# A transformer block's down projection on one core: closing sums moved to GpSimd behind the weights' sums, lower rows first, one scaling operation per row

## The chip, the cores and the metric

The kernel runs on one core of a Trainium2 chip. The metric is device time in microseconds (us). The time before is 1584.97 us, the median of three runs (1581.94 to 1589.53). One further execution was profiled; all durations below come from it. Engines: PE is TensorE's matmul (PEld its weight load), DVE is VectorE, ACT is ScalarE, POOL is GpSimd, SP is SyncE, which here only issues DMAs.

## The reference, cut to what matters

The kernel computes one decoder block for a sequence of 1024 tokens and a model width of 1024: a state-space branch and an attention branch, merged and projected, and then a feed-forward part. The change lies in the last two lines:

```python
h = modulate(rmsnorm(x, norm2_g[l]), sh2, sc2)
ffn = (jax.nn.silu(h @ w_ffn_gate[l]) * (h @ w_ffn_up[l])) @ w_ffn_down[l]
x = x + g2 * ffn
return rmsnorm(x, norm_f_g)
```

The hidden width is 2816, that is 22 blocks of 128. `g2` is one row of 1024 values and is multiplied into the rows of `w_ffn_down`, so that the projection can be added to `x` directly. The final `rmsnorm` scales each row of the output by one number (the reciprocal root of its mean square) and by the row `gf`, which holds `norm_f_g`.

## The kernel before

Only `down` (from line 1164 on) and a few tables above it matter here. Every fp32 matrix product is made of three matmuls: each operand is split into a rounded high part (`h`, cast on ACT) and a rest (`l`, the difference, on DVE), and `PRODUCTS` multiplies high by high, high by rest and rest by high.

**Seven products in place of eight.** The output is cut into four quadrants of 512 rows by 512 columns: upper rows (row tiles 0 to 3, of 128 rows each) and lower rows (4 to 7), left and right columns. Twenty of the hidden blocks are taken in ten pairs. For each pair seven products of sums of blocks replace eight products of blocks. The sums on the activations' side are read from memory (`hD`, line 1203). The sums on the weights' side are made on POOL (line 1211, one operation of 128x512), except for products 2 and 5, which need none. Then come ACT's cast (line 1212, or 1208) and DVE's difference (line 1213, or 1209).

**Three steps.** `STEPS = (4, 3, 3)` deals the ten pairs out over three passes. In each pass the seven products are run in the order `ORDER = (2, 4, 5, 3, 1, 6, 7)`. For one product in the last pass, PE makes four output tiles of nine matmuls each (line 1220), 36 matmuls, and DVE adds each finished tile to that product's accumulator (line 1226). The accumulators are named `pb` (products 4, 5, 7) and `x` (2, 3, 1, 6) in the trace; the listings of instructions number them: `x_9958` and `x_9959` are product 2, `x_9960` and `x_9961` product 3, `x_9962` and `x_9963` product 1, `x_9964` and `x_9965` product 6, two tiles in each.

**The closing sums.** The quadrants are sums of accumulators. In the last pass each product's tiles are followed by the sums that have become possible (line 1230), 32 operations of 128x512:

```python
CLOSE = ((2, 6, 2, ALU.subtract), (4, 2, 4, ALU.add), (4, 7, 4, ALU.add), (5, 7, 5, ALU.subtract),
         (3, 6, 3, ALU.add), (3, 3, 5, ALU.add), (1, 6, 1, ALU.add), (1, 7, 1, ALU.add))
TENG = (6, 7)
```

An entry (z, o, a, op) says: behind product z, accumulator o takes in accumulator a. The entries whose numbers stand in `TENG`, the two that take in product 1, run on DVE, the others on POOL. At the end the upper quadrants are in accumulators 7 and 3, the lower ones in 2 and 6.

**The row loop** (from line 1256 on). The two hidden blocks that are left get four plain operands (lines 440 and 441, `operand`). For each row tile t from 0 to 7, PE makes two tiles of six matmuls (line 1268) and DVE adds each to its quadrant (line 1270). ACT squares the row and sums it (line 1278), POOL multiplies the row by `gf` (line 1251), and `rstd` makes the row's scale from the sum with a few 128x1 operations on DVE (lines 450, 456, 460, 461) and ACT (453, 454). DVE multiplies the row by it (line 1253) and SP writes the row out (line 1254). The scaling of a row is written behind the first half of the next one. The last row does its halves apart (lines 1246 to 1249, 1272 and 1274).

Each engine runs its instructions in a fixed order. A scheduler sets that order when the kernel is built, from the order in the code, the priorities and the buffers; an instruction that waits holds up all behind it on its engine.

Of the kernel before, what the change touches and what calls it, by code (L numbers as in the profile page):

```python
# [9 lines left out]
F32 = mybir.dt.float32  # L10
# [3 lines left out]
ALU = mybir.AluOpType  # L14
# [14 lines left out]
class S5:  # L29
# [244 lines left out]
    def run(self, m, tabs, u_src, y_dst):  # L274
# [55 lines left out]
        for j in range(8):  # L330
# [4 lines left out]
P = 128  # L335
KT = 8
# [24 lines left out]
SIGN_A = {i: ALU.subtract if i in (6, 7) else ALU.add for i in range(1, 8)}  # L361
SIGN_B = {i: ALU.subtract if i in (3, 4) else ALU.add for i in range(1, 8)}

CLOSE = ((2, 6, 2, ALU.subtract), (4, 2, 4, ALU.add), (4, 7, 4, ALU.add), (5, 7, 5, ALU.subtract),
         (3, 6, 3, ALU.add), (3, 3, 5, ALU.add), (1, 6, 1, ALU.add), (1, 7, 1, ALU.add))
SLOT = {3: 0, 6: 1, 7: 2, 4: 3, 1: 4, 2: 5, 5: 6}

BENG = {(i, j, e) for i in range(1, 8) for j in range(2) for e in range(2) if j or not e or i == 6}
# [1 line left out]

STEPS = (4, 3, 3)

TENG = (6, 7)


class Turns:

# [15 lines left out]
class Block:  # L393
# [674 lines left out]
    def gate_up(self, pair, wv, tp):  # L1068
# [3 lines left out]
        for x, y in ((1, 0), (1, 1), (0, 0), (0, 1)):  # L1072
            t = A[x, y] = self.W.tile([P, 2, 4, P], F32, name="wb")
            for q in range(2):
# [87 lines left out]
    def down(self, const, tp, g2, gf):  # L1162

        nc = self.nc
        w_v = self.i["w_ffn_down"][0].rearrange("(m p) n -> m p n", p=P)
        x_v = self.xD.rearrange("(t p) n -> p t n", p=P)
        flat = lambda t: t.rearrange("p a b -> p (a b)")
        L, R = slice(0, 512), slice(512, 1024)
        ring = self.wring + [(self.F, t, t) for t in ("f0", "f0", "f1", "f1")]
        self.turn = 0  # L1170
        acc = {}
        for i in (4, 5, 7, 2, 3, 1, 6):
            pool, tag = (self.PB, "pb") if i in (4, 5, 7) else (self.X, "x1")
            acc[i] = [pool.tile([P, 2, 512], F32, name=tag) for _ in range(2)]
            if i in FROM:
                x, y = FROM[i]
                for a in range(2):
                    nc.sync.dma_start(out=acc[i][a], in_=x_v[:, 4 * x + 2 * a:4 * x + 2 * a + 2, 512 * y:512 * y + 512])
        for i, op in ((5, ALU.add), (4, ALU.subtract)):
            for a in range(2):  # L1180
                nc.gpsimd.tensor_tensor(flat(acc[7][a]), flat(acc[7][a]), flat(acc[i][a]), op)

        def tiles():
            pool, ht, lt = ring[self.turn % len(ring)][0:3]
            self.turn += 1
            return pool.tile([P, 1024], F32R, name=ht), pool.tile([P, 1024], F32R, name=lt)

        def weights(m):
            w = self.PA.tile([P, 1024], F32, name="pa")
            nc.sync.dma_start(out=w, in_=w_v[m])  # L1190
            nc.gpsimd.tensor_tensor(w, w, g2, ALU.mult)  # L1191
            return w

        p0 = 0
        stages = Turns(*[(self.W, "wb", 4)] * 4, *self.stages.pools)
        for s, np_ in enumerate(STEPS):
            W = [(weights(2 * p), weights(2 * p + 1)) for p in range(p0, p0 + np_)]
            for n, i in enumerate(ORDER):
                ops = []
                (ay, ax), b = TERMS_B[i]  # L1200
                for p in range(np_):
                    st = stages.tile([P, 1024], F32)
                    nc.sync.dma_start(out=st[:, L], in_=self.hD[p0 + p, :, SLOT[i]])
                    u = W[p][ay][:, 512 * ax:512 * ax + 512]
                    h, l = tiles()
                    if b is None:
                        for q, v in ((L, st[:, L]), (R, u)):
                            nc.scalar.copy(h[:, q], v)
                            nc.vector.tensor_tensor(l[:, q], v, h[:, q].bitcast(F32), ALU.subtract)  # L1209
                    else:  # L1210
                        nc.gpsimd.tensor_tensor(st[:, R], u, W[p][b[0]][:, 512 * b[1]:512 * b[1] + 512], SIGN_B[i])  # L1211
                        nc.scalar.copy(h, st)
                        nc.vector.tensor_tensor(l, st, h.bitcast(F32), ALU.subtract)  # L1213
                    ops.append((h, l))
                for t in range(4):
                    ps = self.banks.tile([P, 512], F32)
                    j = 0
                    for o in ops:
                        for x, y in PRODUCTS:
                            nc.tensor.matmul(ps, lhsT=o[x][:, P * t:P * t + P], rhs=o[y][:, R], start=(j == 0), stop=(j == 3 * np_ - 1))  # L1220
                            j += 1
                    m = {z: acc[z][t // 2][:, t % 2] for z in acc}
                    if s == 0 and i not in FROM:
                        (nc.scalar.copy if (n * 4 + t) % 2 else nc.vector.tensor_copy)(m[i], ps)
                    else:
                        nc.vector.tensor_tensor(m[i], ps, m[i], ALU.add)  # L1226
                    if s == len(STEPS) - 1:
                        for c, (z, o, a, op) in enumerate(CLOSE):
                            if z == i:
                                (nc.vector if c in TENG else nc.gpsimd).tensor_tensor(m[o], m[o], m[a], op)  # L1230
            p0 += np_
        ops = []
        for m in range(2):
            st = self.W.tile([P, 1024], F32, name="wb", bufs=4)
            nc.sync.dma_start(out=st, in_=self.lD[m])
            ops.append((self.operand(st, tiles=tiles()), self.operand(weights(20 + m), tiles=tiles())))
        out = self.out.rearrange("o (t p) d -> p (o t) d", p=P)
        L, R = slice(0, 512), slice(512, 1024)

        def at(t):  # L1240
            return lambda n: small[:, t, "vya".index(n) + 2:"vya".index(n) + 3]

        def close(t, row, ss):
            if t == 7:
                r = self.rstd(const, ss[:, 1:2], 1, ss[:, 0:1], at(t))
                nc.scalar.mul(row[:, L], row[:, L], r)
                nc.vector.scalar_tensor_tensor(row[:, R], row[:, R], r, gf[:, R], ALU.mult, ALU.mult)
                for cs in (L, R):
                    nc.sync.dma_start(out=out[:, t, cs], in_=row[:, cs])
                return  # L1250
            nc.gpsimd.tensor_tensor(row, row, gf, ALU.mult)
            r = self.rstd(const, ss[:, 0:1], 1, None, at(t))
            nc.vector.tensor_scalar(row, row, r, None, ALU.mult)
            nc.sync.dma_start(out=out[:, t], in_=row)

        small = const.tile([P, KT, 5], F32, name="ss3")
        last = None
        for t in range(KT):
            ss = small[:, t, 0:2]
            row = self.PA.tile([P, 1024], F32, name="pa")  # L1260
            sq = tp.tile([P, 1024], F32, name="ft")
            for c in range(2):
                cs = slice(512 * c, 512 * c + 512)
                ps = self.banks.tile([P, 512], F32)
                j = 0
                for h, w in ops:
                    for x, y in PRODUCTS:
                        nc.tensor.matmul(ps, lhsT=h[x][:, P * t:P * t + P], rhs=w[y][:, cs], start=(j == 0), stop=(j == 5))
                        j += 1
                nc.vector.tensor_tensor(row[:, cs], ps, acc[((7, 3), (2, 6))[t // 4][c]][t % 4 // 2][:, t % 2], ALU.add)  # L1270
                if t == 7:
                    nc.scalar.activation(sq[:, cs], row[:, cs], AF.Square, accum_out=ss[:, c:c + 1])
                    if c == 0:
                        nc.gpsimd.tensor_tensor(row[:, cs], row[:, cs], gf[:, cs], ALU.mult)
                if c == 0 and last:
                    close(*last)
            if t != 7:
                nc.scalar.activation(sq, row, AF.Square, accum_out=ss[:, 0:1])
            last = (t, row, ss)
        close(*last)  # L1280

    def run(self):
        tc, nc, i = self.tc, self.nc, self.i
        with ExitStack() as es:
# [77 lines left out]
            with ExitStack() as s4:  # L1362
                self.X = s4.enter_context(self.pool("x1", KT, side="right"))
                self.F = s4.enter_context(self.pool("f", 4, side="right"))
                self.W = s4.enter_context(self.pool("wb", 4, side="right"))
                wx = s4.enter_context(self.pool("wx", 1, side="right"))
# [44 lines left out]
```

## Time and profile before

| | before |
|---|---|
| median of three runs | 1584.97 us |
| the profiled execution's own time | 1583.8 us |
| its span in the profile | 1582.1 us |
| PE busy | 1424.0 us (90%) |
| DVE busy | 1094.8 us (69%) |
| POOL busy | 821.3 us (52%) |
| ACT busy | 616.2 us (39%) |
| start of the last product's stall on PE | 1519.2 us |
| first add of the row loop on DVE | 1544.77 us |

The span is the stretch from the first to the last thing that the profile recorded; the execution's own time is 1.7 us longer. Busy shares are means over stages with different limits, so the end of the program has to be read from its own stretch, from about 1509 us on. In the rows below a time is counted from the span's start, a duration in a timeline is in us and in a group of instructions in us and in ns, and what stands in square brackets is the idle time of the engine ahead of that row and what ended it.

### The profile page before, as it was taken

Reading aid. Unit: us, or ns where it says so; the run is one execution under the profiler, and the core shown is the slowest. Engines: PE = TensorE matmul, PEld = TensorE weight load, DVE = VectorE, ACT = ScalarE, POOL = GpSimd, SP = SyncE. Lnnn points to the kernel's source line nnn. Section 1 sums busy time; section 2 is a strip of 40 time slices with the busy share of each in tenths; the row PEclk is TensorE's granted clock in tenths of the full one; section 3 lists DMA queues with packets and bytes.
Section 4 is the critical chain, followed back from the end, with each engine's and each line's share of the span. In section 5 each row is a group of like instructions: output and inputs, shape, how many; then the busy total and the mean of one; then the engine's idle time right before and its main releaser. Section 6 shows DMA issues by size and latency. Waiting matters only on the chain.

```text
span 1582.1 us, 18396 instructions
## 1 busy us (share of the span) xinstructions
PE 1424.0 (90%) x6578; PEld 1117.5 (71%) x6578; DVE 1094.8 (69%) x1317; ACT 616.2 (39%) x792; POOL 821.3 (52%) x642
## 2 busy tenths in 40 slices
PE   4898888799998899989799879999999998999965
PEld 2698767678755555647688668888888887787854
DVE  5548777442577787766723986666665669999978
ACT  5431111452565656565315543233323233433313
POOL 2488684010445454532420636554445468879774
PEclk9899999999999999999899989999999999999988
DMA  8456666635423233236334315333333246545302
GB/s 284 161 142 177 179 188 172 182 106 181 132 80 108 81 97 124 94 101 224 114 142 146 107 40 154 106 113 108 106 100 100 93 164 229 151 142 163 102 22 107
DMA packets 180451, 210.46 MB, mean 133 GB/s; under 512 B 28612, under 2 KB 121896, under 8 KB 180360
## 3 DMA queue, kind: packets, MB, share of 16 engines
q1 hardware_dynamic: 169288, 201.29, 40.1%
q10 hardware_dynamic: 11072, 8.00, 1.8%
q8 instruction: 52, 0.85, 0.2%
q14 instruction: 39, 0.32, 0.1%
HBM read 159.18 MB, written 48.89 MB: 132 GB/s over the span
## 4 chain that ended last, share of the span: by engine, by line
PE 30%; DVE 10%; issue 5%; POOL 4%; ACT 1%; DMA 1%; POOLq 0%; DVEq 0%; ACTq 0%
PE tq L1138 11%; PE wo L1138 9%; PE wo L1019 5%; PE gu L1138 3%; POOL pa L1191 1%; DVE f L1213 1%; POOL wb L1211 1%; POOL pb L1230 1%; DVE pb L1226 1%; DVE x L1226 1%; DVE f L1209 1%; DVE wl L1209 1%; DMA pa<-in_w_ffn_down_dram 1%; DVE ft L438 1%; PE tq L1220 0%
## 5 line engine op out<-in xcount | busy, mean ns | idle before, releaser
L438 POOL TENSOR_TENSOR ws<-wb 128x1024 f32<-128x1024 f32 x29 | 73.2, 2524 | 105.7 <-DVE wl L441 59.9
L770 POOL TENSOR_SCALAR wh<-ws 128x1024 fp32r<-128x1024 f32 (+1 forms) x40 | 38.6, 964 | 124.7 <-DVE ws L769 87.9
L422 POOL TENSOR_TENSOR wl<-ws,wh 128x1024 fp32r<-128x1024 f32 x14 | 37.1, 2656 | 116.3 <-ACT wh L419 106.9
L771 DVE TENSOR_TENSOR wl<-ws,wh 128x1024 fp32r<-128x1024 f32 (+1 forms) x40 | 66.1, 1653 | 36.8 <-POOL wh L770 36.7
L438 POOL TENSOR_TENSOR wgs<-wb 128x1024 f32<-128x1024 f32 x15 | 37.9, 2527 | 101.5 <-DVE x L441 35.1
L781 POOL TENSOR_TENSOR wa<-wa,wb 128x1024 f32<-128x1024 f32 (+2 forms) x32 | 67.8, 2120 | 31.8 <-DMA wb<-cD 26.1
L803 ACT ACTIVATE wa<-wa 128x1024 f32<-128x1024 f32 (+1 forms) x40 | 38.9, 972 | 80.3 <-DVE wa L802 75.8
L802 DVE TENSOR_TENSOR wa<-wa,acc 128x512 f32<-128x512 f32 (+1 forms) x80 | 46.8, 623 | 29.9 <-POOL wa L781 26.7
L871 DVE SCALAR_TENSOR_TENSOR acc<-aw,cond,acc 128x512 f32<-128x512 f32 x56 | 54.7, 978 | 18.1 <-DMA aw<-in_w_ada_dram 17.5
L1191 POOL TENSOR_TENSOR pa<-pa,row 128x1024 f32<-128x1024 f32 x22 | 66.3, 3034 | 1.5 <-DMA pa<-in_w_ffn_down_dram 1.5
L769 DVE SCALAR_TENSOR_TENSOR ws<-wa,ws 128x1024 f32<-128x1024 f32 (+1 forms) x40 | 53.4, 1336 | 16.4 <-ACT ws L768 16.3
L1129 POOL TENSOR_TENSOR f<-f,f 128x512 f32<-128x512 f32 x30 | 49.1, 1661 | 26.0 <-DVE f L1119 17.5
L701 PE MATMUL acc<-wh,upto 128*128 128x512 f32 (+1 forms) x80 | 32.7, 409 | 26.9 <-DVE wa L802 26.2
L766 ACT ACTIVATE ws<-wa 128x1024 f32<-128x1024 f32 (+1 forms) x40 | 38.9, 973 | 37.3 <-DVE wa L763 36.6
L419 ACT CAST wh<-ws 128x1024 fp32r<-128x1024 f32 x28 | 29.2, 1047 | 55.0 <-PE wo L1019 30.2
L1211 POOL TENSOR_TENSOR wb<-pa 128x512 f32<-128x512 f32 x23 | 40.2, 1756 | 15.7 <-DVE wxl L1209 5.5
L1118 ACT ACTIVATE f<-f 128x1024 f32<-128x1024 f32 x22 | 23.3, 1061 | 56.5 <-DVE f L1158 29.1
L701 PE MATMUL z<-q,k 64*128 64x512 f32 (+3 forms) x192 | 41.8, 526 | 3.3 <-DVE wa L763 1.7
L701 PEld LDWEIGHTS acc<-wh,upto 128*128 128x128 f32 x80 | 15.5, 194 | 37.9 <-issue 29.7
L1129 POOL TENSOR_TENSOR f<-f 128x512 f32<-128x512 f32 x20 | 42.2, 2126 | 0.0
L1220 PE MATMUL tq<-f,f 128*128 128x512 f32 x96 | 31.1, 407 | 11.8 <-DVE f L1213 11.8
L1220 PE MATMUL wo<-f,f 128*128 128x512 f32 x132 | 40.7, 389 | 0.0
(818 smaller groups left out, 4888.4 us busy)
## 6 DMA issues: line engine op xcount, KB each, us to landing
aw<-in_w_ada_dram SPq DMA_DIRECT2D x32, 512.0 KB
wb<-cD SPq DMA_DIRECT2D x32, 512.0 KB
hD<-f SPq DMA_DIRECT2D x30, 512.0 KB
ws<-in_w_in_dram SPq DMA_DIRECT2D x23, 512.0 KB
wb<-in_w_ffn_gate_dram SPq DMA_DIRECT2D x44, 256.0 KB
wb<-in_w_ffn_up_dram SPq DMA_DIRECT2D x44, 256.0 KB
pa<-in_w_ffn_down_dram SPq DMA_DIRECT2D x22, 512.0 KB
wb<-hD SPq DMA_DIRECT2D x40, 256.0 KB
```

The source lines that it names most:

```text
L438: (add or nc.gpsimd).tensor_tensor(st, a, b, op)
L701: return self.tc.keep_in_program_order(self.nc.tensor.matmul(*args, **kw))
L769: nc.vector.scalar_tensor_tensor(st, a, 0.0, st, ALU.max, ALU.add)
L771: nc.vector.tensor_tensor(lt, st, ht.bitcast(F32), ALU.subtract)
L781: nc.gpsimd.tensor_tensor(a[:, :, o], a[:, :, o], g.behind[:, :, old], ALU.subtract)
L871: nc.vector.scalar_tensor_tensor(acc, w[:, j], cj, acc, ALU.mult, ALU.add)
L1019: nc.tensor.matmul(ps, lhsT=mg[t // 4][k][:, a, P * (t % 4):P * (t % 4) + P], rhs=ws[k // 2][b][:, k % 2], start=(j == 0), stop=(j == 23))
L1129: nc.gpsimd.tensor_tensor(o, a, b, op)
L1138: self.nc.tensor.matmul(ps, lhsT=w[x][:, q, k], rhs=self.B[i](y, k), start=(j == 0), stop=(j == 11))
L1191: nc.gpsimd.tensor_tensor(w, w, g2, ALU.mult)
L1211: nc.gpsimd.tensor_tensor(st[:, R], u, W[p][b[0]][:, 512 * b[1]:512 * b[1] + 512], SIGN_B[i])
L1220: nc.tensor.matmul(ps, lhsT=o[x][:, P * t:P * t + P], rhs=o[y][:, R], start=(j == 0), stop=(j == 3 * np_ - 1))
```

## The change

It touches the tables and `down` alone. `CLOSE` now names, for the position of a product in `ORDER`, the closing sums that are written ahead of that product's matmuls, behind its weights' sums and later than before by one product or more. All 32 run on POOL, tied in order behind the last weights' sum. Accumulator 5 takes in 3, where 3 took in 5, so the upper right quadrant ends in 5. The loads and operands of the two hidden blocks that are left are written ahead of product 7. The row tiles are taken in the order 4, 5, 6, 7, 0, 1, 2, 3. For seven of the eight rows the multiplication by `gf` on POOL and the scaling on DVE become one operation on DVE with the row, the row's scale and `gf` as inputs.

```diff
-CLOSE = ((2, 6, 2, ALU.subtract), (4, 2, 4, ALU.add), (4, 7, 4, ALU.add), (5, 7, 5, ALU.subtract),
-         (3, 6, 3, ALU.add), (3, 3, 5, ALU.add), (1, 6, 1, ALU.add), (1, 7, 1, ALU.add))
+CLOSE = {2: ((6, 2, ALU.subtract),), 3: ((2, 4, ALU.add),), 4: ((7, 4, ALU.add),), 5: ((7, 5, ALU.subtract), (5, 3, ALU.add)),
+         6: ((6, 3, ALU.add), (6, 1, ALU.add)), 7: ((7, 1, ALU.add),)}
-TENG = (6, 7)
+ROWS = (4, 5, 6, 7, 0, 1, 2, 3)
...
+        def closing(n):
+            for t in range(4):
+                for o, a, op in CLOSE.get(n, ()):
+                    o, a = (acc[z][t // 2][:, t % 2] for z in (o, a))
+                    self.after(nc.gpsimd.tensor_tensor(o, o, a, op), last_sum)
...
+            if s == len(STEPS) - 1:
+                WL = [weights(20 + m) for m in range(2)]
...
+                if s == len(STEPS) - 1:
+                    if n == 6:
+                        rest = []
+                        for m in range(2):
+                            st = self.W.tile([P, 1024], F32, name="wb", bufs=4)
+                            nc.sync.dma_start(out=st, in_=self.lD[m])
+                            rest.append((self.operand(st, tiles=tiles()), self.operand(WL[m], tiles=tiles())))
+                    closing(n)
...
-                    if s == len(STEPS) - 1:
-                        for c, (z, o, a, op) in enumerate(CLOSE):
-                            if z == i:
-                                (nc.vector if c in TENG else nc.gpsimd).tensor_tensor(m[o], m[o], m[a], op)
             p0 += np_
-        ops = []
-        for m in range(2):
-            st = self.W.tile([P, 1024], F32, name="wb", bufs=4)
-            nc.sync.dma_start(out=st, in_=self.lD[m])
-            ops.append((self.operand(st, tiles=tiles()), self.operand(weights(20 + m), tiles=tiles())))
+        closing(7)
+        ops = rest
...
-            nc.gpsimd.tensor_tensor(row, row, gf, ALU.mult)
             r = self.rstd(const, ss[:, 0:1], 1, None, at(t))
-            nc.vector.tensor_scalar(row, row, r, None, ALU.mult)
+            nc.vector.scalar_tensor_tensor(row, row, r, gf, ALU.mult, ALU.mult)
...
-        for t in range(KT):
+        for t in ROWS:
...
-                nc.vector.tensor_tensor(row[:, cs], ps, acc[((7, 3), (2, 6))[t // 4][c]][t % 4 // 2][:, t % 2], ALU.add)
+                nc.vector.tensor_tensor(row[:, cs], ps, acc[((7, 5), (2, 6))[t // 4][c]][t % 4 // 2][:, t % 2], ALU.add)
```

**What it does to the order of instructions.** On PE, and on SP's queue, the order stays as it was. On DVE and POOL it stays up to two places near the end, which are shown here. The changed kernel's line numbers differ: 1213 became 1221, 1226 became 1242, 1230 became 1197, 1211 became 1219, 441 became 440, and 1270 became 1278.

First DVE, from the middle operand of product 7 (`f_11527`) to the operands of the row loop; `f_11534` is the rest part of product 7's last operand. Before:

```order
L1213 TENSOR_TENSOR f_11527<-ws,f_11526 128x1024
L1226 TENSOR_TENSOR x_9962<-tq,x_9962 128x512 x2
L1230 TENSOR_TENSOR x_9964<-x_9964,x_9962 128x512
L1230 TENSOR_TENSOR pb<-pb,x_9962 128x512
...
L1226 TENSOR_TENSOR x_9963<-tq,x_9963 128x512
L1213 TENSOR_TENSOR f_11534<-wgs,f_11533 128x1024
```

And in the changed kernel, where the same operand is `f_11528`:

```order
L1221 TENSOR_TENSOR f_11521<-ws,f_11520 128x1024
L1242 TENSOR_TENSOR x_9962<-tq,x_9962 128x512 x2
L1242 TENSOR_TENSOR x_9963<-tq,x_9963 128x512
L1221 TENSOR_TENSOR f_11528<-wgs,f_11527 128x1024
L1242 TENSOR_TENSOR x_9963<-tq,x_9963 128x512
```

Four closing sums stood ahead of product 7's last operand, and four more behind it, among the operands of the row loop; DVE now has none of the eight.

Then POOL, from the last weights' sum (`wgs`, for product 7) to its end. Before:

```order
L1211 TENSOR_TENSOR wgs<-pa 128x512
L1230 TENSOR_TENSOR pb<-pb 128x512 x4
L1230 TENSOR_TENSOR x_9964<-x_9964,x_9960 128x512 x2
L1230 TENSOR_TENSOR x_9965<-x_9965,x_9961 128x512 x2
L1230 TENSOR_TENSOR x_9960<-x_9960,pb 128x512 x2
L1230 TENSOR_TENSOR x_9961<-x_9961,pb 128x512 x2
L1251 TENSOR_TENSOR pa<-pa,gf 128x1024 x7
L1274 TENSOR_TENSOR pa<-pa,gf 128x512
```

In the changed kernel (its last row, the halved multiplication of line 1274, left out):

```order
L1219 TENSOR_TENSOR wgs<-pa 128x512
L1197 TENSOR_TENSOR pb<-pb 128x512 x4
L1197 TENSOR_TENSOR pb<-pb,x_9960 128x512 x2
L1197 TENSOR_TENSOR pb<-pb,x_9961 128x512 x2
L1197 TENSOR_TENSOR x_9964<-x_9964,x_9960 128x512 x2
L1197 TENSOR_TENSOR x_9964<-x_9964,x_9962 128x512
...
L1197 TENSOR_TENSOR x_9965<-x_9965,x_9963 128x512
L1197 TENSOR_TENSOR pb<-pb,x_9962 128x512
...
L1197 TENSOR_TENSOR pb<-pb,x_9963 128x512 x2
```

Behind the last weights' sum POOL had twelve closing sums and seven multiplications of 128x1024; it now has twenty closing sums and none of the multiplications. Ahead of that sum its order is the same in both kernels. The eleventh of the twenty completes the first row tile of accumulator 6, which row tile 4 reads; the thirteenth, fifteenth and seventeenth complete the next three, and the sixteenth, eighteenth, nineteenth and twentieth the four of accumulator 7.

## Rows read from the trace of the kernel before

**Rows 1.** Stretches: busy us of PE, PEld, DVE, ACT, POOL (with instructions), PEclk, DMA.

```profile
1480.00:1509.00 29.00, 29.00 (x129) 24.02 (x129) 29.00 (x28) 8.01 (x8) 29.00 (x16) 1.00 0.36 100
...
1519.00:1531.00 12.00, 0.20 (x1) 0.00 (x0) 8.98 (x7) 0.67 (x1) 12.00 (x9) 0.65 0.00 1
1531.00:1537.00 6.00, 5.99 (x16) 4.72 (x17) 6.00 (x6) 0.00 (x0) 2.77 (x2) 0.56 0.00 0
```

**Rows 2.** Timeline of PE around product 7 (start, us, what).

```profile
1531.01 1.22 PE L1220 MATMUL tq<-f,f 128*128 128x512 f32 x2 [11.81 <-DVE f L1213]
...
1540.15 0.84 PE L1268 MATMUL gu<-f,f 128*128 128x512 f32 x3
```

**Rows 3.** Timeline of DVE from product 7's operands to the row loop.

```profile
1515.81 1.28 DVE L1226 TENSOR_TENSOR x<-tq,x 128x512 f32<-128x512 f32 x2
1522.02 1.73 DVE L1230 TENSOR_TENSOR x<-x,x 128x512 f32<-128x512 f32 x1 [4.93 <-POOL x L1230]
1523.67 1.74 DVE L1230 TENSOR_TENSOR pb<-pb,x 128x512 f32<-128x512 f32 x1
...
1529.27 1.68 DVE L1213 TENSOR_TENSOR f<-wgs,f 128x1024 fp32r<-128x1024 f32 x1
1530.88 0.68 DVE L1226 TENSOR_TENSOR x<-tq,x 128x512 f32<-128x512 f32 x1
...
1534.24 1.21 DVE L441 TENSOR_TENSOR f<-wb,f 128x1024 fp32r<-128x1024 f32 x1
...
1537.11 0.68 DVE L1230 TENSOR_TENSOR x<-x,x 128x512 f32<-128x512 f32 x1
...
1538.31 1.28 DVE L1226 TENSOR_TENSOR x<-wo,x 128x512 f32<-128x512 f32 x2
...
1544.77 0.68 DVE L1270 TENSOR_TENSOR pa<-gu,pb 128x512 f32<-128x512 f32 x1
```

**Rows 4.** Timeline of POOL: last weights' sum, closing sums behind it, first multiplications by `gf`.

```profile
1504.30 2.28 POOL L1230 TENSOR_TENSOR pb<-pb 128x512 f32<-128x512 f32 x1
...
1513.50 1.29 POOL L1211 TENSOR_TENSOR wgs<-pa 128x512 f32<-128x512 f32 x1
1514.76 6.00 POOL L1230 TENSOR_TENSOR pb<-pb 128x512 f32<-128x512 f32 x4
1520.72 5.81 POOL L1230 TENSOR_TENSOR x<-x,x 128x512 f32<-128x512 f32 x4
1526.50 7.27 POOL L1230 TENSOR_TENSOR x<-x,pb 128x512 f32<-128x512 f32 x4
1547.31 4.76 POOL L1251 TENSOR_TENSOR pa<-pa,gf 128x1024 f32<-128x1024 f32 x2 [13.54 <-ACT ft L1278]
```

**Rows 5.** Groups of instructions, 1470 to 1582 us: the row loop's scalings on DVE.

```profile
L1253 DVE TENSOR_SCALAR pa<-pa,ss 128x1024 f32<-128x1024 f32 x7 | 7.3, 1044 | 0.0
L461 DVE TENSOR_TENSOR ss<-ss 128x1 f32<-128x1 f32 x8 | 7.1, 892 | 0.2
L456 DVE SCALAR_TENSOR_TENSOR ss<-ss 128x1 f32<-128x1 f32 x8 | 6.4, 800 | 0.0
```

**Rows 6.** Timeline of DVE in the row loop: the same operations, one of them held up.

```profile
1549.95 2.13 DVE L461 TENSOR_TENSOR ss<-ss 128x1 f32<-128x1 f32 x1
...
1552.60 0.74 DVE L1253 TENSOR_SCALAR pa<-pa,ss 128x1024 f32<-128x1024 f32 x1
...
1553.92 0.20 DVE L456 SCALAR_TENSOR_TENSOR ss<-ss 128x1 f32<-128x1 f32 x1
...
1554.35 0.16 DVE L461 TENSOR_TENSOR ss<-ss 128x1 f32<-128x1 f32 x1
```

**Rows 7.** Timeline of DVE, an earlier stage: a three-input operation of 128x1024.

```profile
704.66 1.21 DVE L769 SCALAR_TENSOR_TENSOR ws<-wa,ws 128x1024 f32<-128x1024 f32 x1
```

**Rows 8.** Timeline of ACT: the cast of product 7's last operand, and the program's last operation.

```profile
1514.83 1.05 ACT L1212 CAST f<-wgs 128x1024 fp32r<-128x1024 f32 x1 [0.20 <-POOL wgs L1211]
...
1577.69 0.72 ACT L1246 ACTIVATE pa<-pa,ss 128x512 f32<-128x512 f32 x1 [0.93 <-DVE ss L461]
```

More of the change, by code (lines that the diff above doesn't have):

```diff
@@ L1192, in weights @@
             return w
+        def closing(n):
[3 more added lines that the diff above has]
+                    self.after(nc.gpsimd.tensor_tensor(o, o, a, op), last_sum)
         p0 = 0
+        last_sum = None
         stages = Turns(*[(self.W, "wb", 4)] * 4, *self.stages.pools)
@@ L1210, in down @@
                     else:
-                        nc.gpsimd.tensor_tensor(st[:, R], u, W[p][b[0]][:, 512 * b[1]:512 * b[1] + 512], SIGN_B[i])
+                        last_sum = nc.gpsimd.tensor_tensor(st[:, R], u, W[p][b[0]][:, 512 * b[1]:512 * b[1] + 512], SIGN_B[i])
                         nc.scalar.copy(h, st)
@@ L1243, in close @@
         def close(t, row, ss):
-            if t == 7:
+            if t == ROWS[-1]:
                 r = self.rstd(const, ss[:, 1:2], 1, ss[:, 0:1], at(t))
@@ L1269, in down @@
                         j += 1
-                nc.vector.tensor_tensor(row[:, cs], ps, acc[((7, 3), (2, 6))[t // 4][c]][t % 4 // 2][:, t % 2], ALU.add)
-                if t == 7:
+                nc.vector.tensor_tensor(row[:, cs], ps, acc[((7, 5), (2, 6))[t // 4][c]][t % 4 // 2][:, t % 2], ALU.add)
+                if t == ROWS[-1]:
                     nc.scalar.activation(sq[:, cs], row[:, cs], AF.Square, accum_out=ss[:, c:c + 1])
@@ L1276, in down @@
                     close(*last)
-            if t != 7:
+            if t != ROWS[-1]:
                 nc.scalar.activation(sq, row, AF.Square, accum_out=ss[:, 0:1])
```

## The prediction, made before the changed kernel was run

> **What bounds the kernel now.** The page gives PE 90% of the span, but that is a mean over stages, and PE, DVE and POOL carry the same instructions in the same order in both kernels until about 1515 us. So I read only the end, first by stretches. From 1480 to 1509 us PE, DVE and POOL are all busy without a gap. From 1519 to 1531 us PE does 0.20 us of work while POOL works all 12 [rows 1]. PE's timeline names the wait: 11.81 us, until DVE has made the rest part of product 7's last operand [rows 2]. DVE's timeline tells why that came so late: it was not slow, it stood in line. Behind the adds that end at 1517.09, DVE takes up a closing sum that waits 4.93 us for POOL, then three more of them, 1.65 to 1.67 us from one to the next, an add, and only at 1529.27 the operand [rows 3]. POOL meanwhile works through the sums that came due behind its last weights' sum [rows 4]. After 1531 us DVE is busy without a gap up to the row loop (starting 1544.77), and PE, at a granted clock of 0.56 in the first 6 us [rows 1] (near the lower level, 1.2 of 2.4 GHz, behind 11.81 us in which it stood idle; 1.00 before), is not what is waited for. The row loop then ends with ACT's operation at 1577.69 + 0.72 = 1578.41 [rows 8]; what follows until 1582.1 is the write of the last row, which stays. So the end is DVE's list, from 1517 us on.
>
> **One price first: what POOL and DVE cost each other.** A 128x512 sum of two SBUF tiles on DVE follows the one before after 0.60 us if POOL is idle (1537.11, the first of two that end at 1538.31), and after 1.65 when POOL is summing [rows 3]: it loses 1.05 us to each POOL operation it meets. POOL's own 128x512 sums follow each other after 1.25 us at best (1513.50 to 1514.76, and 6.00 for the next four with one wait of about 1 us among them) [rows 4]. Adds that read PSUM lose nothing (0.68 us throughout). I take 1.25 us for a POOL sum alone and a wait of at most 1.05 for either side, and not POOL's recorded durations of up to 2.28, which hold its own waiting.
>
> **Step 1, eight closing sums leave DVE.** The operand of product 7 then follows one PSUM add (0.60) behind 1517.09. Its inputs are there: the weights' sum ends at 1514.79 [rows 4] and ACT's cast at 1515.88 [rows 8]. The operand takes 1.13 us alone (1.21 with the part that the next one overlaps) and a wait between 0 and 1.05, so it ends near 1519.4 instead of 1530.95: **11.5 us earlier**. PE waits well under 1 us; that it keeps its clock I count at nothing, because DVE, not PE, sets what comes next. From the operand to the row loop DVE now takes 1544.77 - 1530.88 = 13.9 us. Four closing sums in it take 2.76 (from 1531.48, 0.60 behind the add at 1530.88, to 1534.24) and 1.20 (1537.11 to 1538.31) [rows 3]; without them 9.9 are left. Before, POOL had run dry by then (its twelfth sum ends at 1533.77). Now it hasn't, and each of the four operands of line 441 will meet it: I take 0.6 for each, 2.5 in all (bounds 0 and 4.2). The row loop starts on DVE at 1519.4 + 9.9 + 2.5 = 1531.8, **13.0 us earlier** than 1544.77. PE ends product 7 near 1527 and is ready for it.
>
> **Step 2, the row loop's own work.** It took 1578.41 - 1544.77 = 33.6 us. The multiplications by `gf` on POOL, 2.4 us each [rows 4], make DVE wait: eight operations of line 461 took 7.1 us where one alone takes 0.16, eight of line 456 took 6.4 against 0.20, and seven of line 1253 took 7.3 against 0.74 [rows 5, 6]. That is 5.8 + 4.8 + 2.1 = 12.7 us, which go, and 20.9 are left. The joint scaling costs 1.21 us, by an earlier stage's operation of the same kind and size [rows 7], against 0.74: seven times 0.47 is 3.3 more. **24.2 us.**
>
> **Step 3, the closing sums come back in the row loop.** POOL has twenty sums from about 1515.8 us (DVE holds it up by 1 us at first). The eleventh completes what row tile 4 needs: 11 x 1.25 = 13.75, and five waits for DVE's operands of about 0.95, so 1534.3; DVE would be ready at 1532.4 and waits **1.9 us**. The nine that follow take 11.3 us, and the first scalings put them off by a few more, to about 1549. Rows come at 3.0 us (24.2 over eight) and need two sums each (2.5), so POOL keeps up, but DVE's small operations and scalings meet it: nine sums at about half of 1.05 make **some 4 us**. The row loop takes 24.2 + 1.9 + 4.0 = 30.1, **3.5 us less**. Were no sum in the way it would be 24.2.
>
> The row order costs nothing by itself: the first four rows read accumulators 2 and 6, which are complete first, and it hides four rows' time over the sums for accumulator 7. The earlier loads and operands of the two remaining blocks don't move any instruction on PE, SP or ACT's casts: nothing. That the closing sums are written behind the weights' sums also changes nothing ahead of the last one; what changes is only whose list they are in.
>
> **Sum.** 13.0 + 3.5 = 16.5 us. The profiled execution took 1583.8 us and would take 1567.3; the median of the three runs lies 1.2 above it, so the forecast is **1568.5 us**, 1.0% faster. Its bounds: with no new waits at all (2.5 + 5.9 back) 1560; with all four operands at 1.05 and all nine sums at 1.05, 1.7 + 5.4 less, 1575.6.
>
> **Rival A: POOL's twenty sums become the bound.** If each took the 2.28 us that the slowest recorded ones took [rows 4], the last would be there at 1514.8 + 45.6 = 1560.4. The last row tile then still has its adds, its square and its scale, about 7 us: 1567.5 instead of 1578.4, a gain of 11, and **1574 us**. For it: no resource is used more in that stretch. Against: 2.28 was reached only where DVE had an SBUF sum or difference between any two of POOL's; in the row loop it mostly reads PSUM.
>
> **Rival B: the port, at its full price; the other side.** What DVE loses per POOL sum is the decisive number. I count 8.4 us over the twenty, 0.42 each. At 1.05 for every one, the most that [rows 3] show, 21 are lost, 12.6 more: **1581 us**, no change. From (8.4 + 16.5)/20 = 1.25 us each the gain is gone, and from (24.9 + 7.9)/20 = 1.64 the kernel is slower by more than 0.5%. At 2 us, which is what line 461 lost to one of POOL's 128x1024 operations (2.13 against 0.16 [rows 6]), 40 are lost and it takes **1600 us**. The Trainium skill (SBUF — State Buffer, "SBUF: two separate sides") states the rule behind it: whichever of a two-input DVE operation and a GpSimd operation starts first holds the shared ports for its whole instruction, and the other fully blocks. By that rule and the recorded 1.82 us of POOL's last four sums the loss would come near the 2 us and the time near the 1600; that DVE lost 1.05 to a sum so recorded speaks against taking the whole duration. Against the rival: the sums are half as long as the operations that cost 2 us, and of DVE's operations on a row only three take two SBUF tiles.
>
> **Rival C: the stall has another cause.** If product 7's last operand waited for POOL's weights' sum or ACT, freeing DVE would save only the row loop's part, 3.5 us: 1581.5, no change. Against: the weights' sum had ended at 1514.79, 14.5 us ahead of the operand, and DVE was the engine without a gap from 1522.
>
> **How the numbers follow.** Some 0.5% (7.9 us) is what a measurement of this kernel can tell from no change; its three runs spread over 7.6. Forecast with its bounds: 0.71. Rival A: 0.14, still faster. Rival B at 1.05 a sum: 0.08, rival C: 0.03, both within 0.5%. Rival B from 1.64: 0.04. So faster 0.85, same 0.11, slower 0.04. The range goes from 1563 (half of the new waits gone, and a low draw among the runs) to 1578, which takes in rival A; 0.04 of the forecast's own chance lies below and rivals B and C above.
>
> **What would show it.** In the profile after: PE with no wait over 1 us in product 7 and granted clock 1.00 through it; the operand's difference ending near 1519.4 of a span that is the same up to there; the first add of the row loop near 1531.8; one wait of DVE for POOL of about 2 us at row tile 4; twenty closing sums ending near 1549; the joint scaling at 1.21 to 1.3 us where POOL is idle; the last operation near 1562. A row loop of over 36 us, or closing sums that run past 1555, would make it wrong, as would a difference ahead of 1515 us.

## The result, and the profile after

The changed kernel takes 1567.33 us (median of four runs, 1565.95 to 1567.69), beside 1584.38 us for the kernel before (four runs). The ratio is 0.9886, 95% interval 0.9867 to 0.9905: faster by 1.1%. The forecast was 1568.5 us, 1.0% faster, with a range of 1563 to 1578.

The stretches of the changed kernel, with the columns of [rows 1]: start:end, length, busy us of PE, PEld, DVE, ACT and POOL with their instructions, the granted clock, DMA share and GB/s.

```profile
1519.00:1531.00 12.00, 9.63 (x38) 7.62 (x37) 12.00 (x13) 0.00 (x0) 12.00 (x7) 0.91 0.00 1
1531.00:1537.00 6.00, 6.00 (x25) 4.89 (x24) 3.02 (x7) 1.68 (x5) 6.00 (x6) 0.90 0.01 3
1537.00:1545.00 8.00, 8.00 (x37) 6.60 (x37) 7.90 (x13) 2.99 (x8) 8.00 (x7) 1.00 0.17 67
1545.00:1555.00 10.00, 6.48 (x29) 5.05 (x27) 10.00 (x24) 5.71 (x14) 1.84 (x1) 1.00 0.37 150
```

From 1519 to 1531 us PE now works 9.63 us, where it worked 0.20. Its timeline, as [rows 2], has two waits left in the whole end of the program:

```profile
1518.64 0.72 PE L1236 MATMUL tq<-f,f 128*128 128x512 f32 x2 [0.24 <-DVE f L1221]
...
1528.80 0.79 PE L1276 MATMUL gu<-wl,wh 128*128 128x512 f32 x1 [2.37 <-DVE wl L440]
```

The 11.81 us in front of product 7's last operand are 0.24; the 2.37 us are for the last operand of the row loop. DVE's timeline, as [rows 3], shows why: the operand (line 1221, at 1516.80) stands directly behind the three adds, and the row loop's operands (line 440) and adds fill the time to the row loop, which starts at 1531.06.

```profile
1515.00 1.88 DVE L1242 TENSOR_TENSOR x<-tq,x 128x512 f32<-128x512 f32 x3
1516.80 1.79 DVE L1221 TENSOR_TENSOR f<-wgs,f 128x1024 fp32r<-128x1024 f32 x1
1518.51 0.68 DVE L1242 TENSOR_TENSOR x<-tq,x 128x512 f32<-128x512 f32 x1
1519.11 1.71 DVE L440 TENSOR_TENSOR f<-wb,f 128x1024 fp32r<-128x1024 f32 x1
1520.74 2.31 DVE L440 TENSOR_TENSOR f<-pa,f 128x1024 fp32r<-128x1024 f32 x1
...
1531.06 0.67 DVE L1278 TENSOR_TENSOR pa<-gu,x 128x512 f32<-128x512 f32 x1
1533.65 1.29 DVE L1278 TENSOR_TENSOR pa<-wo,x 128x512 f32<-128x512 f32 x2 [1.92 <-POOL x L1197]
...
1537.61 1.03 DVE L460 TENSOR_TENSOR ss<-ss 128x1 f32<-128x1 f32 x1
...
1543.41 2.27 DVE L1261 SCALAR_TENSOR_TENSOR pa<-pa,ss,gf 128x1024 f32<-128x1024 f32 x1
...
1548.22 1.28 DVE L1261 SCALAR_TENSOR_TENSOR pa<-pa,ss,gf 128x1024 f32<-128x1024 f32 x1
```

The last rows show what the closing sums still cost in the row loop: a wait of 1.92 us at row tile 4, then a 128x1 operation of 1.03 us that takes 0.16 alone, and a joint scaling of 2.27 us that takes 1.28 once POOL is done. POOL's timeline, as [rows 4], has the twenty sums in a row, from 1513.95 to 1546.85:

```profile
1512.69 1.30 POOL L1219 TENSOR_TENSOR wgs<-pa 128x512 f32<-128x512 f32 x1
1513.95 8.02 POOL L1197 TENSOR_TENSOR pb<-pb 128x512 f32<-128x512 f32 x4
1521.92 7.95 POOL L1197 TENSOR_TENSOR pb<-pb,x 128x512 f32<-128x512 f32 x4
1529.84 8.78 POOL L1197 TENSOR_TENSOR x<-x,x 128x512 f32<-128x512 f32 x7
1538.59 1.29 POOL L1197 TENSOR_TENSOR pb<-pb,x 128x512 f32<-128x512 f32 x1
1539.83 2.28 POOL L1197 TENSOR_TENSOR x<-x,x 128x512 f32<-128x512 f32 x1
1542.07 4.78 POOL L1197 TENSOR_TENSOR pb<-pb,x 128x512 f32<-128x512 f32 x3
```

Where DVE's operands alternate with POOL's sums, a sum comes every 2 us on average (8.02 and 7.95 for four). Where DVE mostly reads PSUM, every 1.25 us (8.78 for seven).

**A measure that leaves the scatter out.** Runs of one kernel scatter: the kernel before took 1574.72 to 1586.93 us in twenty runs on one chip. The traces show where that arises. In the ten profiled executions the last operation of an earlier stage (the three-input operation of line 769; 768 or 767 in the others) starts between 700.0 and 708.8 us; from there to POOL's last weights' sum it is 806.9 to 809.8 us in all of them. All of that lies ahead of the change, and the instructions there stand in the same order. So beside the times I use the **tail**: from the start of POOL's last weights' sum (line 1211; 1219 or 1218 in the others) to the end of ACT's last operation. It was 1578.41 - 1513.50 = 64.9 us before and is 1562.09 - 1512.69 = 49.4 us after: 15.5 us less.

### The profile page after: what moved, and what is told of

Read it like the earlier page. It is cut to its first block, busy times and chain, and to the rows that moved or that the text cites. A ratio compares the mean times of both kernels' runs of the same rounds, so it can differ in the third digit from the quotient of the medians.

```text
span 1566.0 us, 18381 instructions
## 1 busy us (share of the span) xinstructions
PE 1420.6 (91%) x6578; PEld 1113.9 (71%) x6578; DVE 1076.0 (69%) x1309; ACT 615.5 (39%) x792; POOL 820.9 (52%) x643
## 4 chain that ended last, share of the span: by engine, by line
PE 26%; DVE 10%; issue 7%; POOL 6%; DMA 2%; ACT 1%; SPq 0%; DVEq 0%; POOLq 0%; ACTq 0%
PE tq L1137 10%; PE wo L1137 8%; PE wo L1018 5%; PE gu L1137 3%; POOL pb L1197 1%; POOL pa L1190 1%; DVE f L1221 1%; DMA pa<-in_w_ffn_down_dram 1%; POOL wb L1219 1%; DVE pb L1242 1%; DVE x L1242 1%; POOL x L1197 1%; DVE f L1217 1%; DVE wl L1217 1%; DVE ft L437 1%
## 5 line engine op out<-in xcount | busy, mean ns | idle before, releaser
L770 DVE TENSOR_TENSOR wl<-ws,wh 128x1024 fp32r<-128x1024 f32 (+1 forms) x40 | 62.0, 1551 | 36.8 <-POOL wh L769 36.7
L801 DVE TENSOR_TENSOR wa<-wa,acc 128x512 f32<-128x512 f32 (+1 forms) x80 | 46.8, 623 | 34.2 <-POOL wa L780 34.2
L700 PEld LDWEIGHTS acc<-wh,upto 128*128 128x128 f32 x80 | 15.5, 193 | 40.0 <-issue 29.3
L700 PE MATMUL mm<-wa,V 128*64 128x512 f32 (+3 forms) x192 | 39.8, 507 | 0.4 <-ACT wa L802 0.4
```

Of the source, the lines that this page charges most:

```text
L700: return self.tc.keep_in_program_order(self.nc.tensor.matmul(*args, **kw))
L770: nc.vector.tensor_tensor(lt, st, ht.bitcast(F32), ALU.subtract)
L801: nc.vector.tensor_tensor(a[:, x, 0:f], a[:, x, 0:f], r[:, x, 0:f], ALU.subtract)
```

## The experiments

All are compared with the kernel before on their own chip: e1 to e4 with a median of 1580.36 us (twenty runs), the repeat of the changed kernel and e5 to e7 with 1579.56 (seventeen). The table gives each profiled execution's marks, in us from its span's start; the row loop is counted from its first add to the last operation. The ratio is the recorded one; it differs from the quotient of the two medians by up to 0.0015.

| kernel | last weights' sum | first add of the row loop | last operation ends | tail | row loop | time, median | ratio to before (95%) |
|---|---|---|---|---|---|---|---|
| before | 1513.50 | 1544.77 | 1578.41 | 64.9 | 33.6 | 1584.38 | 1 |
| changed | 1512.69 | 1531.06 | 1562.09 | 49.4 | 31.0 | 1567.33 | 0.9886 (0.9867 to 0.9905) |
| e1, sums only | 1513.31 | 1531.68 | 1575.72 | 62.4 | 44.0 | 1578.76 | 0.9982 (0.9962 to 1.0002) |
| e2, scaling only | 1518.66 | 1549.94 | 1575.69 | 57.0 | 25.7 | 1573.72 | 0.9966 (0.9944 to 0.9987) |
| e3, upper rows first | 1506.86 | 1534.06 | 1560.39 | 53.5 | 26.3 | 1566.03 | 0.9920 (0.9895 to 0.9945) |
| e4, sixteen sums left out | 1511.54 | 1528.86 | 1554.60 | 43.1 | 25.7 | 1560.36 | 0.9877 (0.9851 to 0.9903) |
| changed, again | 1511.00 | 1529.37 | 1560.41 | 49.4 | 31.0 | 1567.28 | 0.9907 (0.9887 to 0.9928) |
| e5, product 1 on DVE | 1512.90 | 1542.88 | 1567.70 | 54.8 | 24.8 | 1568.68 | 0.9927 (0.9904 to 0.9950) |
| e6, sums by need | 1509.55 | 1527.49 | 1557.40 | 47.9 | 29.9 | 1562.90 | 0.9884 (0.9861 to 0.9907) |
| e7, eight more sums | 1508.15 | 1526.53 | 1565.00 | 56.9 | 38.5 | 1573.93 | 0.9956 (0.9939 to 0.9974) |

The tails repeat: 49.4 us in both executions of the changed kernel. The other kernels have one profiled execution each, but stretches that they share agree: from the last weights' sum to the row loop it is 18.37 or 18.38 us in the changed kernel, its repeat, e1 and e7, and 31.27 and 31.28 in the kernel before and e2. Where a difference of a few us is in question, the tail decides; the ratios' intervals are 3 to 4 us wide to either side, and each holds what the tail says.

For the repeat a tail of 49.4 within 0.5 had been expected, and a time 15 to 17 us under the kernel before. The tail came so. The medians lie only 12.3 us apart, though the interval of the ratio, 11 to 18 us, does not rule the expectation out. So the 17.1 us between the medians of the first comparison hold some scatter.

**e1: the sums moved, the scalings left apart.** On the changed kernel:

```diff
-            r = self.rstd(const, ss[:, 0:1], 1, None, at(t))
-            nc.vector.scalar_tensor_tensor(row, row, r, gf, ALU.mult, ALU.mult)
+            nc.gpsimd.tensor_tensor(row, row, gf, ALU.mult)
+            r = self.rstd(const, ss[:, 0:1], 1, None, at(t))
+            nc.vector.tensor_scalar(row, row, r, None, ALU.mult)
```

> The changed kernel with a row's two scalings apart again (POOL multiplies by gf, DVE by the row's scale). The account from the prediction, in which the two parts need each other: POOL's multiplications now queue behind the twenty closing sums, which end at 1546.9 us in the changed kernel, so the first row's scaling on DVE waits until about 1549; from that scaling to the last operation the kernel before took 25.8 us (1552.60 to 1578.41), so the last operation comes near 1575 and the time is about 1580, only 3 to 5 us under the kernel before. Rival, the parts are independent: the stall's 13 us are gained whatever the scaling does, and the time is about 1571. In both PE has no wait over 1 us in product 7.

The tail is 62.4 us, 2.5 less than before, and the time cannot be told from the kernel before. The stall of PE is gone here too (the row loop starts 18.4 us behind the last weights' sum, as in the changed kernel), but the row loop takes 44.0 us. DVE's timeline of this kernel:

```profile
1539.17 0.68 DVE L1279 TENSOR_TENSOR pa<-tq,x 128x512 f32<-128x512 f32 x1
1547.86 2.82 DVE L1262 TENSOR_SCALAR pa<-pa,ss 128x1024 f32<-128x1024 f32 x1 [8.01 <-POOL pa L1260]
...
1553.69 1.69 DVE L455 SCALAR_TENSOR_TENSOR ss<-ss 128x1 f32<-128x1 f32 x1
...
1555.60 2.12 DVE L460 TENSOR_TENSOR ss<-ss 128x1 f32<-128x1 f32 x1
```

The first row's scaling waits 8.01 us for POOL's multiplication, which stands behind the twenty sums, and the port waits of [rows 5, 6] follow as before. So moving the sums to POOL pays in full only because POOL loses the multiplications. The rival of independent parts (1571 us) falls.

**e2: the joint scaling alone.** On the kernel before, the same three lines the other way round.

> The kernel before with the joint scaling alone. The account from the prediction: the 11.8 us stall of PE in product 7 and the row loop's start at 1544.8 stay; with no POOL operation in the row loop its 33.6 us lose the 12.7 us of waits at the port and gain seven times 0.5: about 24.3 us, 9.4 less, time about 1575. Rival, the joint scaling is worth what the row loop gained in the changed kernel, 2.6 us: 1582. Rival, the 128x1 operations were slow for another reason than POOL's multiplications (ACT's answers came late): they stay at 0.8 to 0.9 us mean and the joint scaling only costs 3.5: 1588.

The tail is 57.0 us, 7.9 less than before. PE's stall is there unchanged (11.80 us for the same operand). The groups of DVE in the row loop, to be read against [rows 5]:

```profile
L1252 DVE SCALAR_TENSOR_TENSOR pa<-pa,ss,gf 128x1024 f32<-128x1024 f32 x7 | 9.0, 1279 | 0.0
...
L461 DVE TENSOR_TENSOR ss<-ss 128x1 f32<-128x1 f32 x8 | 2.3, 291 | 0.1
L456 DVE SCALAR_TENSOR_TENSOR ss<-ss 128x1 f32<-128x1 f32 x8 | 1.7, 211 | 0.0
```

The 128x1 operations fall from 892 and 800 ns to 291 and 211: they were slow because of POOL's multiplications, not of ACT. The joint scaling takes 1.28 us. The row loop is 25.7 us, where 24.3 had been expected, and neither rival fits. Apart, the two parts of the change give 2.5 and 7.9 us; together they give 15.5.

**e3: upper rows first.** On the changed kernel `ROWS = (0, 1, 2, 3, 4, 5, 6, 7)`.

> The changed kernel with the row tiles in the order 0 to 7. Theory: row tile 0 now reads first what POOL's sixteenth sum completes (at 1539.9 in the changed kernel), so DVE's first add of the row loop comes at about 1540 instead of 1531.1; after that only the last four sums meet DVE, and the row loop from there takes about 26 us instead of 31: last operation near 1566, time about 1571, 4 us over the changed kernel. Rival, the order of the rows is nothing because POOL keeps ahead of the rows either way: 1567.

The tail is 53.5 us, 4.1 more than in the changed kernel, as expected. DVE's timeline has the wait at the first row:

```profile
1534.06 0.69 DVE L1278 TENSOR_TENSOR pa<-gu,pb 128x512 f32<-128x512 f32 x1 [8.75 <-POOL pb L1197]
```

Of the 8.75 us half come back, because the rows behind it meet few sums: the row loop is 26.3 us. The median of 1566.03 looks like the rival's 1567, but this execution's last weights' sum came 5.8 us earlier than the changed kernel's, ahead of anything that differs. The order of the rows is worth 4 us in this kernel, though it moves no work.

**e4: sixteen closing sums left out.** On the changed kernel the entries (5, 3), (6, 3), (6, 1) and (7, 1) are taken out of `CLOSE`.

> The changed kernel without its last sixteen closing sums (5 takes in 3, 6 takes in 3 and 1, 7 takes in 1), so that part of the output's sums is left out; nothing else differs. It prices what the closing sums cost in the row loop. Theory: without them the row loop needs 24.2 us and no wait for POOL, and the operands ahead of it lose about 1.5 us less at the port: row loop from about 1529.5, last operation near 1553.7, time about 1559, 8 us under the changed kernel. Rival, the row loop is bound by DVE's and ACT's exchange and the sums hardly matter: 1565 or more.

The tail is 43.1 us, 6.3 less than in the changed kernel (8 had been expected). The row loop is 25.7 us, the same as in e2, which had no sums in its row loop either. That is what the row loop takes without sums, 1.5 us more than the 24.2 of the prediction. The start of the row loop comes 17.3 us behind the last weights' sum in place of 18.4. DVE's timeline shows where the 1.5 us can lie:

```profile
1532.82 0.69 DVE L1277 TENSOR_TENSOR pa<-tq,x 128x512 f32<-128x512 f32 x1 [0.16 <-PE tq L1275]
...
1539.62 0.69 DVE L1277 TENSOR_TENSOR pa<-wo,pb 128x512 f32<-128x512 f32 x1 [0.30 <-PE wo L1275]
...
1543.70 0.69 DVE L1277 TENSOR_TENSOR pa<-tq,pb 128x512 f32<-128x512 f32 x1 [0.24 <-PE tq L1275]
1544.31 1.28 DVE L1260 SCALAR_TENSOR_TENSOR pa<-pa,ss,gf 128x1024 f32<-128x1024 f32 x1
...
1548.99 1.23 DVE L459 TENSOR_TENSOR ss<-ss 128x1 f32<-128x1 f32 x1
```

The last row's halved multiplication by `gf` stays on POOL and holds one small operation up to 1.23 us (1.1 more than alone), the joint scaling takes 1.28 and not 1.21 (seven times, 0.5), and DVE waits for PE three times, 0.70 us together. In e5, below, PE is ahead of the row loop, which has no sums and no wait for PE there and takes 24.8 us. So PE's lateness is worth about 0.9 of the 1.5, and 0.6 are left for the other two, which were not measured apart.

**e5: product 1's sums on DVE, at the new places.** On the changed kernel:

```diff
-                for o, a, op in CLOSE.get(n, ()):
+                for k, (o, a, op) in enumerate(CLOSE.get(n, ())):
                     o, a = (acc[z][t // 2][:, t % 2] for z in (o, a))
-                    self.after(nc.gpsimd.tensor_tensor(o, o, a, op), last_sum)
+                    (nc.vector.tensor_tensor(o, o, a, op) if n == 7 or (n == 6 and k) else self.after(nc.gpsimd.tensor_tensor(o, o, a, op), last_sum))
```

> The changed kernel with the eight closing sums that take in product 1 on DVE again, at the places where the changed code writes them (behind product 7's operands). POOL has twelve sums behind the last weights' sum. Theory, the port and DVE's list decide: PE's stall in product 7 stays away, but DVE waits for POOL's sums of 6 and 3 ahead of the row loop's operands and does eight sums more in a list without gaps: the first add of the row loop comes 8 to 12 us later than in the changed kernel, the row loop gets back 5 of them (25.7 us, as without sums), and the tail is 53 to 56 us. Rival, the place behind the operands is the whole gain and the engine doesn't matter: tail 49 to 50.

The tail is 54.8 us, 5.4 more than in the changed kernel and inside the 53 to 56 that had been expected. PE has no stall in product 7 (0.26 us), so the place alone removes that. But the stall comes back one stage later. PE's timeline:

```profile
1537.35 0.80 PE L1276 MATMUL gu<-wl,wh 128*128 128x512 f32 x1 [10.71 <-DVE wl L440]
```

And DVE's, which had waited ahead of that operand:

```profile
1529.36 3.40 DVE L1197 TENSOR_TENSOR x<-x,x 128x512 f32<-128x512 f32 x2 [4.33 <-POOL x L1197]
...
1542.88 0.68 DVE L1278 TENSOR_TENSOR pa<-gu,x 128x512 f32<-128x512 f32 x1
```

The row loop starts 11.6 us later and then takes 24.8, with no POOL sum left in it. The engine matters: a sum on DVE that waits for POOL stands ahead of operands that don't need it.

**e6: POOL's sums in the order of need.** On the changed kernel:

```diff
-CLOSE = {2: ((6, 2, ALU.subtract),), 3: ((2, 4, ALU.add),), 4: ((7, 4, ALU.add),), 5: ((7, 5, ALU.subtract), (5, 3, ALU.add)),
-         6: ((6, 3, ALU.add), (6, 1, ALU.add)), 7: ((7, 1, ALU.add),)}
+CLOSE = {2: ((6, 2, ALU.subtract),), 3: ((2, 4, ALU.add),), 4: ((7, 4, ALU.add),), 5: ((6, 3, ALU.add),),
+         6: ((6, 1, ALU.add),), 7: ((7, 5, ALU.subtract), (7, 1, ALU.add), (5, 3, ALU.add))}
```

> The changed kernel with POOL's last twenty sums in the order in which they are needed: 6 takes in 3 ahead of product 6's adds, then 1; all that rows 0 to 3 read (7 and 5) behind them. Theory: row tile 4 no longer waits for the eleventh sum (1.92 and 0.43 us of waits gone), POOL meets the row loop's operands somewhat less and the row loop somewhat more (twelve sums in place of nine, about 0.45 us each): 1 to 3 us less, tail 46.5 to 48.5. Rival, the waits at row tile 4 only move to a later row: tail 49 to 50.

The tail is 47.9 us, 1.5 less than in the changed kernel. DVE has no wait for POOL's sums:

```profile
1527.49 0.68 DVE L1278 TENSOR_TENSOR pa<-gu,x 128x512 f32<-128x512 f32 x1
1528.09 1.34 DVE L1278 TENSOR_TENSOR pa<-wo,x 128x512 f32<-128x512 f32 x2
```

The row loop gets 1.1 us shorter, not by the 2.4 us of the waits, and it now meets twelve sums in place of nine. The time of 1562.90 us (four runs) is the lowest of all the complete kernels, but of the 4.4 us to the changed kernel on the same chip the tail holds 1.5. Another 1.5 lie ahead of the last weights' sum (1509.55 beside 1511.00), where nothing differs; the rest was not traced.

**e7: eight more sums.** On the changed kernel position 7 of `CLOSE` becomes `((7, 1, ALU.add), (7, 1, ALU.subtract), (7, 1, ALU.add))`.

> The changed kernel with eight more closing sums: accumulator 7 takes in product 1, gives it back and takes it in again, so POOL has twenty-eight sums behind the last weights' sum. Where POOL's row of sums becomes the bound (rival A of the prediction): row tile 0's first add waits for the twenty-fifth sum, about 6 us, and the tail is 55 to 58. If a sum costs only what it takes from DVE at the port, about 0.45 us each: tail 53. If POOL's sums cost nothing in the row loop: 49 to 50.

The tail is 56.9 us, 7.5 more. DVE's timeline:

```profile
1541.08 0.68 DVE L1278 TENSOR_TENSOR pa<-tq,x 128x512 f32<-128x512 f32 x1
1547.33 0.69 DVE L1278 TENSOR_TENSOR pa<-gu,pb 128x512 f32<-128x512 f32 x1 [5.00 <-POOL pb L1197]
```

With twenty-eight sums POOL's list is the bound at row tile 0 (5.00 us of waiting); with twenty it isn't, there is no wait at that place in the changed kernel. So rival A was at most eight sums away.

## Why the prediction was right, point by point

- **What bounds the end.** Right. The stall of PE was DVE's queueing, and freeing DVE of its sums ended it: 0.24 us. Rival C falls with the changed kernel itself, and e2 keeps the stall as it was.
- **Step 1.** Right. Against the last weights' sum the operand was done at 17.45 us before and at 5.90 after, 11.55 earlier (11.5 predicted). From the next add to the row loop it is 1531.06 - 1518.51 = 12.6 us (12.4 predicted), and the row loop starts 12.9 us earlier (13.0 predicted). That product 7 runs at a full clock is right too; that PE would then be ready was a little off, since it waits 2.37 us for the row loop's last operand, beside DVE's path.
- **Step 2.** The direction was right, the size off: without sums the row loop takes 25.7 us (e2 and e4), not 24.2. The step put PE's lateness at nothing, which is worth about 0.9 us (24.8 in e5, where PE is ahead). It took all of the port waits of [rows 5] as gone, though the last row's multiplication stays on POOL and holds one operation up by 1.1, and took [rows 7]'s 1.21 us for a joint scaling of 1.28; these two share the other 0.6.
- **Step 3.** Nearly right: the sums cost the row loop 31.0 - 25.7 = 5.3 us (5.9 predicted), among them the wait at row tile 4 at 1.92 us (1.9 predicted) and a second of 0.43 that was not foreseen. The twenty sums end 34.2 us behind the start of the last weights' sum (35.5 predicted).
- **The sum.** 12.9 + 2.6 = 15.5 us in the tail, where 16.5 were predicted. The measured medians lie 17.1 us apart; the profiled executions' part ahead of the tail differs by 0.8 us by chance, and the interval of the ratio (15 to 21 us) holds 15.5. The row loop's total came within 0.9 us of the forecast partly because step 2 counted 1.5 too little and step 3 counted 0.6 too much. That the time came out 1.2 us below the forecast, though the gain was 1.0 smaller, is luck, the scatter of the runs.
- **"The row order costs nothing by itself."** That held as it was put, for the order chosen, but it hid a term: the other order would have cost 4.1 us (e3).
- **"The earlier loads and operands of the two remaining blocks don't move any instruction on PE, SP or ACT's casts."** The traces agree: ACT's first cast of these operands starts 2.29 us behind the last weights' sum in both kernels (1515.79 before, 1514.98 after).
- **"That the closing sums are written behind the weights' sums also changes nothing ahead of the last one."** Right for POOL. For DVE the place alone would have moved the stall from product 7 to the row loop (e5).
- **Rival B.** The decisive number was DVE's loss per sum. Twenty sums cost 5.3 in the row loop and 12.6 - 9.9 = 2.7 ahead of it: 0.40 us each (0.42 counted; the gain would have gone at 1.25). A single operation of DVE lost up to 1.1 us to POOL's sums (2.31 against the 1.21 of [rows 3] ahead of the row loop, 2.27 against 1.28 in it), never the 2 us that the 128x1024 multiplications cost. The Trainium skill's rule of the port (SBUF — State Buffer, "SBUF: two separate sides"), by which one side blocks while the other works, agrees with the trace: the 128x1 operation that started at 1537.61 ended at 1538.64, and the POOL sum beside it at 1538.62. What the prediction put into that rule was POOL's recorded 1.82 us; but recorded durations of up to 2.28 hold POOL's own waiting, and a sum beside which DVE mostly read PSUM took 1.25. The Trainium skill's advice to time GpSimd's operations by the spacing of their starts (Perfetto Trace Analysis, "GPSIMD Engine Instruction") changes little here: the sum at 1538.59, recorded with 1.29 us, is followed after 1.24, and the one at 1539.83, recorded with 2.28, after 2.24.

## What to carry to other kernels

In an engine's fixed list an operation costs what it waits for, charged to everything behind it: look at what stands behind a waiting instruction before looking at how long it takes, and give work that has to wait to an engine whose list holds nothing urgent behind it. Two edits on the same two engines may not add up: here they gave 2.5 and 7.9 us alone and 15.5 together, because one freed the time that the other filled. When runs scatter by more than the effect, find where the scatter arises and measure from behind it.

## What the runs showed of the hardware that was not expected

Behind a wait of some 2.4 us PE's clock fell in some executions and not in another. In the changed kernel the granted clock is 1.00 up to 1526 us, and behind the wait of 2.37 us it is 0.60, near the lower level (1.2 of 2.4 GHz):

```profile
1518.00:1526.00 8.00, 7.76 (x34) 6.11 (x33) 8.00 (x8) 0.88 (x1) 8.00 (x5) 1.00 0.00 1
...
1529.00:1533.00 4.00, 4.00 (x12) 3.17 (x13) 2.73 (x5) 0.00 (x0) 4.00 (x4) 0.60 0.00 0
```

Its matmuls then follow each other after 0.43 us in place of 0.23 for some 3 us. In e1, too, the clock fell behind a wait of 2.35 us, to 0.76 over 1530 to 1537 us. In e3 the same wait was 2.35 us as well and ended at 1522.97, and the clock stayed at the upper level:

```profile
1523.00:1527.00 4.00, 4.00 (x18) 3.30 (x19) 2.31 (x4) 0.00 (x0) 4.00 (x4) 1.00 0.00 0
```

Before, behind a wait of 1.29 us that ended at 1542.51, it stayed at 1.00 (1537 to 1545 us). Why it fell in one execution and not in the other no run here shows. It cost nothing in the changed kernel, since DVE set the pace: DVE worked without a gap up to 1531.73 and then waited for POOL.
